# Rewriting a two-layer trunk: feature-major inputs, one feed-forward pass, norms spread between matmuls

## The chip, the cores and the metric

The kernel runs on all 8 cores of one Trainium2 chip (two dies of four cores); each core computes its own tokens and nothing is exchanged. The time is that of the slowest core, in device microseconds (us). Most executions agree within 0.3%. Some fall in a slower state, in which one die shows a lower granted TensorE clock (after's run of 1534.13 us: die 0 at 0.81 to 0.83, die 1 at 0.94 to 0.95); these are marked slow and are left out of every comparison here, or only the cores of the undisturbed die are used. PE is TensorE, PEld its weight loads, DVE VectorE, ACT ScalarE, POOL GpSimd.

## The reference

One step of a diffusion trunk with two layers. Each core has 512 prompt tokens (two requests of 256) and a run of some 1,280 latent tokens with its margins; later stages need fewer of them (1,152, then 1,024).

```python
D_MODEL = 1024; D_FF = 2816; DEPTH = 2; BLOCK = WINDOW = CHUNK = 128

def modulate(x, g, shift, scale):
    return rms_norm(x, g) * (1 + scale) + shift

def conv_ffn(h, w_up, conv_w, w_down):
    z = dwconv3(h @ w_up, conv_w)            # 3 taps along the tokens
    g, val = jnp.split(z, 2, axis=-1)
    return (jax.nn.silu(g) * val) @ w_down

def gmlp_mixer(h, w_in, v_g, w_s, b_s, w_out):
    u, v = jnp.split(jax.nn.gelu(h @ w_in), 2, axis=-1)
    v = rms_norm(v, v_g)                     # then mixed in chunks of 128 tokens
    ...
    return (u * s) @ w_out

# for each layer l:
#   shift, scale, gate (x2) = silu(cond) @ ada_w[l] + ada_b[l]      "modulation maps"
#   layer 0: q,k,v, a short gated conv; windowed attention with sink; out-projection
#   layer 1: gmlp_mixer
#   x = x + gate * mixer(modulate(x, ...))
#   x = x + gate2 * conv_ffn(modulate(x, ...), ...)
```

## The kernel before

Activations are kept feature-major in SBUF, the memory on the core (features on the 128 partitions, 8 chunks of them, tokens along the row). x comes token-major from the host, so TensorE transposes it block by block, and the outputs too:

```python
P.dma("sp", st[0:nt, :], dram(dsrc.ap()[roff + t0:roff + t1, :]))
for half in range(2):
    b = bank()
    for kk in range(4):
        k = half * 4 + kk
        P.transpose(b[:, kk * 128:kk * 128 + nt], st[0:nt, k * 128:(k + 1) * 128], ident[0:nt, 0:nt])
    # ... copy to xT
```

Phases end in a fence: everything after it depends on the last operation of every engine and on all transfers before it. A norm is a stage of its own inside such a phase. For each tile of tokens: squares on ScalarE, the sum over features by a matmul with a matrix of ones, and for each of the 8 chunks a product (x times 1/rms) and an affine (scale and shift):

```python
def norm_mod_batched(l, which, ranges, sqs, rstd_all, tmps, part="both"):
    # ... squares, sums, Ln and Exp for every tile, then for each tile:
        for k in range(KC):
            tm = tmps[(k % 2) * 2 + (k // 2) % 2]
            if k % 2 == 0:
                P.tt("dve", tm[:, 0:n], xT[:, k, xc:xc + n], rs, ALU.mult)
                P.act(hT[:, k, hc:hc + n], tm[:, 0:n], AF.Identity,
                      bias=mod_ap(l, 3 * which, k, j), scale=gmod[:, l, which, k:k + 1, j])
            else:
                P.tt("pool", tm[:, 0:n], xT[:, k, xc:xc + n], rs, ALU.mult)
                P.ts("dve", hT[:, k, hc:hc + n], tm[:, 0:n], gmod[:, l, which, k:k + 1, j],
                     mod_ap(l, 3 * which, k, j), ALU.mult, ALU.add)
```

Feed-forward runs twice over the up weights, once for each set of at most 900 columns:

```python
for si, st in enumerate(sts):              # two sets of tiles
    for s in range(nslab):                 # up weights read again for each set
        # ... per tile: 8 + 8 matmuls (gate, value), then
        P.act(tg[:, 0:n], bg[:, 1:n + 1], AF.Identity, scale=fcw[:, l, j, 1:2])
        P.act(tv[:, 0:n], bv[:, 1:n + 1], AF.Identity, scale=fcw[:, l, NFC + j, 1:2])
        P.stt("dve", tg[:, 0:n], bg[:, 0:n], fcw[:, l, j, 0:1], tg[:, 0:n], ALU.mult, ALU.add)
        # ... three more taps on VectorE
        if pending is not None:
            stage_b(pending)               # Silu on ScalarE, gate * value on GpSimd
```

Of the kernel before, what the change touches and what calls it, by code (L numbers as in the profile page):

```python
# [12 lines left out]

ENGINES = ("pe", "act", "dve", "pool", "sp")

class Acc:
    __slots__ = ("ap", "name", "box")

    def __init__(self, ap, name, box):
        self.ap = ap  # L20
        self.name = name
        self.box = box

class T:
    def __init__(self, handle, name, shape, psum=False):
        self.h = handle
        self.name = name
        self.shape = tuple(shape)
        self.psum = psum

    def __getitem__(self, idx):
        if not isinstance(idx, tuple):
            idx = (idx,)
        box = []
        for d, n in enumerate(self.shape):
            if d < len(idx):
                s = idx[d]
                if isinstance(s, slice):
                    lo = 0 if s.start is None else s.start
                    hi = n if s.stop is None else s.stop  # L40
                    assert s.step in (None, 1)
                else:
                    lo, hi = s, s + 1
            else:
                lo, hi = 0, n
            assert 0 <= lo < hi <= n, (self.name, idx, self.shape)
            box.append((lo, hi))
        if self.psum:
            return Acc(self.h[idx], self.name, None)
        return Acc(self.h[idx], self.name, tuple(box))  # L50
# [4 lines left out]
def reg(acc_like, ap):  # L55
    return Acc(ap, acc_like.name, acc_like.box)

def dram(ap):
    return Acc(ap, "dram:", None)
# [6 lines left out]

def _covers(b1, b2):
# [4 lines left out]

class Op:
    __slots__ = ("idx", "eng", "emit", "deps", "is_dma", "sig", "sem", "semval", "waits")

    def __init__(self, idx, eng, emit, is_dma):
# [3 lines left out]
        self.deps = set()  # L80
        self.is_dma = is_dma
# [3 lines left out]
        self.waits = None  # L85

class Prog:
    def __init__(self, nc):
        self.nc = nc
        self.ops = []  # L90
        self.track = {}
        self.final_dmas = []
        self.fence_deps = set()
        self.fence_last = {}
        self.fence_start = 0

    def fence(self):
        last = dict(self.fence_last)
        dmas = set()
        for op in self.ops[self.fence_start:]:  # L100
            if op.is_dma:
                dmas.add(op.idx)
            else:
                last[op.eng] = op.idx
        self.fence_last = last
        self.fence_deps = set(last.values()) | dmas
        self.fence_start = len(self.ops)

    def add(self, eng, emit, reads=(), writes=(), is_dma=False):
        op = Op(len(self.ops), eng, emit, is_dma)  # L110
        self.ops.append(op)
        op.deps |= self.fence_deps
        reads = [a for a in reads if not a.name.startswith("dram:")]
        writes = [a for a in writes if not a.name.startswith("dram:")]
        for a in list(reads):
            if a.box is None:
                reads.remove(a)
                writes.append(a)
        writes = [Acc(a.ap, a.name, ((0, 1),)) if a.box is None else a for a in writes]
        for a in reads:  # L120
            lst = self.track.setdefault(a.name, [])
            for (box, oi, isw) in lst:
                if isw and _overlap(box, a.box):
                    op.deps.add(oi)
            lst.append((a.box, op.idx, False))
        for a in writes:
            lst = self.track.setdefault(a.name, [])
            keep = []
            for ent in lst:
                box, oi, isw = ent  # L130
# [3 lines left out]
                if _overlap(box, a.box):  # L134
                    op.deps.add(oi)
                    if _covers(a.box, box):
                        continue
                keep.append(ent)
            keep.append((a.box, op.idx, True))
            self.track[a.name] = keep  # L140
        op.deps.discard(op.idx)
        return op
# [5 lines left out]
    def transpose(self, out, in_, ident):  # L148
        return self.add("pe", lambda e: e.transpose(out.ap, in_.ap, ident.ap),  # L149
                        reads=[in_, ident], writes=[out])  # L150

    def act(self, out, in_, func, bias=None, scale=None, accum_out=None):
        reads = [in_]
        kw = {}
        if bias is not None:
            if isinstance(bias, Acc):
                reads.append(bias)
                kw["bias"] = bias.ap
            else:
                kw["bias"] = bias  # L160
        if scale is not None:
            if isinstance(scale, Acc):
                reads.append(scale)
                kw["scale"] = scale.ap
            else:
                kw["scale"] = scale
# [9 lines left out]
    def ts(self, eng, out, in0, s1, s2, op0, op1=None):  # L176
        reads = [in0]
        a1, a2 = s1, s2
        if isinstance(s1, Acc):
            reads.append(s1)  # L180
            a1 = s1.ap
        if isinstance(s2, Acc):
            reads.append(s2)
            a2 = s2.ap
        if op1 is None:
            return self.add(eng, lambda e: e.tensor_scalar(out.ap, in0.ap, a1, a2, op0), reads=reads, writes=[out])
        return self.add(eng, lambda e: e.tensor_scalar(out.ap, in0.ap, a1, a2, op0, op1), reads=reads, writes=[out])  # L187
# [15 lines left out]
    def recip(self, out, in_):  # L203
        return self.add("dve", lambda e: e.reciprocal(out.ap, in_.ap), reads=[in_], writes=[out])  # L204

# [3 lines left out]
    def dma(self, q, out, in_, final=False):  # L209
        op = self.add(q, lambda e: e.dma_start(out.ap, in_.ap), reads=[in_], writes=[out], is_dma=True)  # L210
        if final:
# [3 lines left out]
    def lower(self, sems):  # L215
        ops = self.ops
        per_eng = {e: [] for e in ENGINES}
        for op in ops:
            per_eng[op.eng].append(op)
        waited = {e: {} for e in ENGINES}  # L220
        waited_dma = {e: set() for e in ENGINES}
        for op in ops:
            need_c = {}
            need_d = []
            for d in op.deps:
                p = ops[d]
                if p.is_dma:
                    if d not in waited_dma[op.eng]:
                        need_d.append(d)
                else:  # L230
                    if p.eng == "pe" and op.eng == "pe" and not op.is_dma:
                        continue
                    if need_c.get(p.eng, -1) < d:
                        need_c[p.eng] = d
            w = []
            for pe_, d in need_c.items():
                if waited[op.eng].get(pe_, -1) >= d:
                    continue
                waited[op.eng][pe_] = d
                w.append(d)  # L240
            for d in sorted(need_d):
                waited_dma[op.eng].add(d)
                w.append(d)
            op.waits = w
            for d in w:
                ops[d].sig = True
        for op in ops:
            if op.is_dma:
                op.sig = True
        cnt = {e: 0 for e in ENGINES}  # L250
        dma_rr = {e: 0 for e in ENGINES}
        dma_cnt = {}
        dma_last = {}
        pre_wait = {}
        for op in ops:
            if not op.sig:
                continue
            if op.is_dma:
                pool = sems["dma_" + op.eng]
                k = dma_rr[op.eng] % len(pool)  # L260
                dma_rr[op.eng] += 1
                key = (op.eng, k)
                if key in dma_last:
                    pre_wait[op.idx] = dma_last[key]
                dma_cnt[key] = dma_cnt.get(key, 0) + 16
                op.sem = pool[k]
                op.semval = dma_cnt[key]
                dma_last[key] = (op.sem, op.semval)
            else:
# [3 lines left out]
        self.pre_wait = pre_wait  # L273
        self.per_eng = per_eng
        self.stats = {e: len(per_eng[e]) for e in ENGINES}
        self.stats["sig"] = dict(cnt)

    def emit_engine(self, eng_name, e):
        ops = self.ops
        for op in self.per_eng[eng_name]:  # L280
            if op.idx in self.pre_wait:
                s, v = self.pre_wait[op.idx]
                e.wait_ge(s, v)
            for d in op.waits:
                p = ops[d]
                e.wait_ge(p.sem, p.semval)
# [3 lines left out]
        if eng_name == "sp":  # L290
            for op in self.final_dmas:
                e.wait_ge(op.sem, op.semval)

# [21 lines left out]

D = 1024
KC = 8
NS_IN = 1281
NS_QA = 1280
NS_X1 = 1153  # L320
NS_F0 = 1152
NS_G1 = 1152
NS_F1 = 1024
NPR = 256
EPS = 1e-6
DFF = 2816
NFC = 22

class Seg:
    def __init__(self, name, xc0, hc0, n, cond, vb0):  # L330
        self.name = name
        self.xc0 = xc0
        self.hc0 = hc0
        self.n = n
        self.cond = cond
        self.vb0 = vb0

SEG_S = Seg("s", 0, 1, NS_IN, 0, 0)
SEG_P0 = Seg("p0", NS_IN, NS_IN + 3, NPR, 1, 11)
SEG_P1 = Seg("p1", NS_IN + NPR, NS_IN + 3 + NPR + 2, NPR, 1, 13)  # L340
SEGS = [SEG_S, SEG_P0, SEG_P1]
XC = NS_IN + 2 * NPR
HC = NS_IN + 2 + 2 * (NPR + 2)
NVB = 15
SLOT_G = (0, 2, 1, 3)

def split(n, maxw):
    k = -(-n // maxw)
    base = n // k
    rem = n % k  # L350
    out = []
    t = 0
    for i in range(k):
        w = base + (1 if i < rem else 0)
        out.append((t, t + w))
        t += w
    return out

def seg_tiles(ranges, maxw):
    out = []  # L360
    for seg, n in ranges:
# [994 lines left out]
```

## Time and profile before

1686.21 us, median of 4 runs (1683.61 to 1691.12); all eight cores lie between 1671.3 and 1689.6.

| stage of the kernel before (slowest core) | from, to (us) | us | TensorE busy | granted clock |
|---|---|---|---|---|
| layer 0 up to its feed-forward | 0 to 617 | 617 | 407 | 0.75 |
| feed-forward 0 | 617 to 1016 | 399 | 381 | 0.97 |
| layer 1 mixer with both norms | 1016 to 1285 | 269 | 169 | 0.84 |
| feed-forward 1 | 1285 to 1661 | 376 | 355 | 0.97 |
| output transposes and stores | 1661 to 1690 | 29 | 15 | 0.80 |

These are the windows view of the trace, cut at stage boundaries. In the two feed-forwards TensorE is busy for 381 of 399 and 355 of 376 us at clock 0.97, so there little can be won but by fewer columns; in the first and third rows it is without a matmul for 210 and 100 us, and the prediction reads them more finely. What it calls cold starts shows in the same trace: after 32.05 us of idle time TensorE's matmuls had a granted clock of 0.50 from 1062 to 1066 us, and 1.00 from 1068 on.

### The profile page before, as it was taken

Reading aid. Unit: us, or ns where it says so; the run is one execution under the profiler, and the core shown is the slowest. Engines: PE = TensorE matmul, PEld = TensorE weight load, DVE = VectorE, ACT = ScalarE, POOL = GpSimd, SP = SyncE. Lnnn points to the kernel's source line nnn. Section 1 sums busy time; section 2 is a strip of 40 time slices with the busy share of each in tenths; the row PEclk is TensorE's granted clock in tenths of the full one; section 3 lists DMA queues with packets and bytes.
Section 4 is the critical chain, followed back from the end, with each engine's and each line's share of the span. In section 5 each row is a group of like instructions: output and inputs, shape, how many; then the busy total and the mean of one; then the engine's idle time right before and its main releaser. Section 6 shows DMA issues by size and latency. Waiting matters only on the chain.

```text
span 1689.6 us, 29214 instructions; the slowest of 8 cores (1671.3 to 1689.6 us)
## 1 busy us (share of the span) xinstructions
PE 1326.6 (79%) x9098; PEld 843.4 (50%) x9118; DVE 904.7 (54%) x1690; ACT 728.0 (43%) x1468; POOL 463.9 (27%) x506
## 2 busy tenths in 40 slices
PE   2432658979987957999999991886845899999996
PEld 2320226632222733556677770543523566777775
DVE  3135223566765655971799514124447683489812
ACT  1153444246654453640566306468054461256501
POOL 1025420013330232440344203113124342244400
PEclk9985668975555977999999996899887899999998
DMA  9995003315653048657835160320307756964153
GB/s 183 194 143 70 0 1 51 51 18 84 101 100 51 2 54 115 101 76 102 123 64 76 24 97 0 82 51 1 51 0 88 120 87 91 125 96 79 26 69 150
DMA packets 128321, 126.55 MB, mean 75 GB/s; under 512 B 4513, under 2 KB 107689, under 8 KB 128170
## 3 DMA queue, kind: packets, MB, share of 16 engines
q0 software_dynamic: 121392, 108.93, 44.4%
q1 hardware_dynamic: 6778, 15.76, 2.8%
q8 instruction: 76, 1.25, 0.3%
q14 instruction: 75, 0.61, 0.1%
HBM read 226.79 MB, written 6.82 MB: 138 GB/s over the span
## 4 chain that ended last, share of the span: by engine, by line
PE 58%; DMA 15%; DVE 10%; issue 8%; ACT 7%; POOL 1%; DVEq 0%; SPq 0%; ACTq 0%; POOLq 0%
PE ps_b L145 57%; DMA sb_wslab<-w_up 7%; DVE sb_hT L187 3%; DMA sb_xst<-xs 3%; DMA sb_xst<-xp 1%; DVE sb_tq L204 1%; PE ps_b L149 1%; DVE sb_tmpf L195 1%; DMA sb_wslab<-ada_w 1%; ACT sb_junk L171 1%; DMA sb_wdn<-w_down 1%; DVE sb_tg L174 1%; ACT sb_tq L171 1%; DMA ys<-sb_yst 1%; DVE sb_tmpa L174 1%
## 5 line engine op out<-in xcount | busy, mean ns | idle before, releaser
L145 PE MATMUL ps_b<-sb_hT,sb_wslab 128*128 128x258 bf16 (+7 forms) x4520 | 678.4, 314 | 103.1 <-ACT sb_hT L171 61.6
L145 PEld LDWEIGHTS ps_b<-sb_hT,sb_wslab 128*128 128x128 bf16 x4520 | 450.7, 100 | 326.4 <-issue 137.5
L195 DVE SCALAR_TENSOR_TENSOR sb_tmpf<-ps_b,sb_fcw,sb_tmpf 128x256 f32<-128x256 f32 (+3 forms) x880 | 450.8, 547 | 102.2 <-ACT sb_tmpf L171 55.2
L171 ACT ACTIVATE sb_tmpf<-ps_b,sb_fcw 128x256 f32<-128x256 f32 (+3 forms) x440 | 232.0, 528 | 343.6 <-PE ps_b L145 207.2
L174 POOL TENSOR_TENSOR sb_actT<-sb_tmpf,sb_tmpf 128x256 bf16<-128x256 f32 (+3 forms) x220 | 190.7, 867 | 316.1 <-ACT sb_tmpf L171 222.1
L145 PE MATMUL ps_b<-sb_actT,sb_wdn 128*128 128x256 bf16 (+3 forms) x1760 | 242.4, 301 | 4.2 <-DMA sb_wdn<-w_down 2.3
L145 PEld LDWEIGHTS ps_b<-sb_actT,sb_wdn 128*128 128x128 bf16 x1760 | 172.1, 98 | 74.1 <-issue 5.7
L195 DVE SCALAR_TENSOR_TENSOR sb_xT<-ps_b,sb_modv,sb_xT 128x256 f32<-128x256 f32 (+5 forms) x168 | 88.0, 539 | 216.6 <-PE ps_b L145 216.6
L171 ACT ACTIVATE sb_PT<-ps_b 128x256 bf16<-128x256 f32 x308 | 100.0, 382 | 65.4 <-PE ps_b L145 61.6
L171 ACT ACTIVATE sb_tmpf<-sb_tmpf 128x256 f32<-128x256 f32 (+3 forms) x220 | 101.2, 460 | 2.3 <-DVE sb_tmpf L195 2.3
L204 DVE RECIPROCAL sb_tq<-ps_b 64x512 f32<-64x512 f32 x20 | 67.2, 3360 | 38.8 <-PE ps_b L145 38.7
L174 POOL TENSOR_TENSOR sb_PT<-sb_PT,sb_masks 128x512 bf16<-128x512 bf16 (+1 forms) x38 | 43.8, 1154 | 140.6 <-PE ps_b L145 76.9
L171 ACT ACTIVATE sb_hT<-sb_tmpa,sb_modv,sb_gmod 128x256 bf16<-128x256 f32 (+7 forms) x88 | 56.3, 640 | 59.3 <-DVE sb_tmpa L174 58.3
L149 PE MATMUL ps_b<-sb_ident,sb_xst 128*128 128x128 f32 (+1 forms) x120 | 28.1, 412 | 60.3 <-DMA sb_xst<-xs 44.0
L210 POOL DMA_DIRECT2D sb_wdn<-w_down x16 | 21.9, 1367 | 154.5 <-PE ps_b L145 149.7
L145 PE MATMUL ps_b<-sb_wslab,sb_hT 128*128 128x512 bf16 (+2 forms) x322 | 54.9, 329 | 0.3
L149 PEld LDWEIGHTS ps_b<-sb_ident,sb_xst 128*128 128x128 f32 (+1 forms) x120 | 22.9, 223 | 64.1 <-issue 64.1
L204 DVE RECIPROCAL sb_ssq<-sb_ssq 128x1 f32<-128x1 f32 x13 | 2.1, 164 | 92.8 <-ACT sb_ssq L171 92.8
L171 ACT ACTIVATE sb_sqb<-sb_xT 128x2560 bf16<-128x2560 f32 (+3 forms) x9 | 20.3, 2291 | 65.3 <-issue 64.2
L145 PE MATMUL ps_b<-sb_mixT,sb_wslab 128*128 128x288 bf16 (+2 forms) x384 | 48.0, 287 | 0.0
L145 PE MATMUL ps_b<-sb_uT,sb_wslab 128*128 128x384 bf16 (+1 forms) x320 | 47.7, 313 | 0.0
L145 PE MATMUL ps_b<-sb_PT,sb_Vtok 128*128 128x512 bf16 (+1 forms) x68 | 39.5, 582 | 8.9 <-ACT sb_PT L171 7.1
(163 smaller groups left out, 1184.9 us busy)
## 6 DMA issues: line engine op xcount, KB each, us to landing
sb_wslab<-w_up POOLq DMA_DIRECT2D x40, 1024.0 KB, 13.7
sb_wslab<-ada_w POOLq DMA_DIRECT2D x12, 2048.0 KB, 17.1
sb_wdn<-w_down POOLq DMA_DIRECT2D x16, 1408.0 KB, 14.3
sb_xst<-xs SPq DMA_DIRECT2D x10, 512.0 KB, 9.1
sb_wslab<-w_up POOLq DMA_DIRECT2D x8, 512.0 KB, 6.9
sb_wslab<-w_in_odd POOLq DMA_DIRECT2D x2, 2048.0 KB, 20.1
ys<-sb_yst SPq DMA_DIRECT2D x8, 512.0 KB, 2.7
sb_wslab<-w_in_even POOLq DMA_DIRECT2D x6, 512.0 KB, 9.1
```

What stands on the lines that cost most here:

```text
L145: return self.add("pe", lambda e: e.matmul(out.ap, lhsT.ap, rhs.ap, start=start, stop=stop), reads=[lhsT, rhs], writes=[out])
L149: return self.add("pe", lambda e: e.transpose(out.ap, in_.ap, ident.ap), reads=[in_, ident], writes=[out])
L171: return self.add("act", lambda e: e.activation(out.ap, in_.ap, func, **kw), reads=reads, writes=writes)
L174: return self.add(eng, lambda e: e.tensor_tensor(out.ap, in0.ap, in1.ap, op), reads=[in0, in1], writes=[out])
L187: return self.add(eng, lambda e: e.tensor_scalar(out.ap, in0.ap, a1, a2, op0, op1), reads=reads, writes=[out])
L195: return self.add(eng, lambda e: e.scalar_tensor_tensor(out.ap, in0.ap, sc, in1.ap, op0, op1), reads=reads, writes=[out])
L204: return self.add("dve", lambda e: e.reciprocal(out.ap, in_.ap), reads=[in_], writes=[out])
L210: op = self.add(q, lambda e: e.dma_start(out.ap, in_.ap), reads=[in_], writes=[out], is_dma=True)
```

## The change

Its intent: take away what keeps TensorE empty (transposes, norm stages, fences, the second reading of the up weights), so that it runs from one projection to the next.

The diff has 2,616 lines and is a rewrite. SP is the tile of the prompt, S0 to S3 are the latent tiles; the modulation maps are read and computed in slices (`ada`), like the weights. Its core:

```diff
-    def fence(self):                       # all engines, all transfers
+    # dependencies per buffer and range; no fences
...
-    P.transpose(b[:, kk * 128:kk * 128 + nt], st[0:nt, ...], ident[...])
+    P.dma("sp", xP.whole(), dr(d_xp.ap()))      # x, k cache, outputs feature-major in DRAM
...
-    P.recip(den[64:128, :], OD[64:128, :])
+    P.act(d[:, 0:w], d[:, 0:w], AF.Ln)
+    P.act(d[:, 0:w], d[:, 0:w], AF.Exp, scale=-1.0)
...
+    def unit(key, shape, src, at=None):    # weights: slices, contiguous per partition,
+        ...                                # through one ring of 40,960 bytes a partition, in program order
+    for m in (2, 3, 4):
+        ada_units(0, m)
+    for c in range(8):
+        unit(("we", c), [128, KC, 128], d_we.ap()[c])
...
-    norm_mod_batched(...)                  # a stage of its own
+    def queue_apply(nm):
+        side.append(nm.fin)                # Ln, Exp: 1/rms
+        for k in range(KC):
+            side.append(lambda k=k: nm.apply(k, E1[k], E2[k]))   # product, then affine
+
+    E1 = ("dve", "pool", "dve", "pool", "dve", "dve", "pool", "dve")
+    E2 = ("act", "dve", "act", "act", "act", "dve", "act", "act")
+
+    def emit(f, nside=0):                  # one item of matmul work
+        cur = lag[:]
+        del lag[:]
+        f()
+        for c in cur:                      # what the item before left behind: norm sums
+            c()
+        for _ in range(nside):             # and nside steps of a waiting norm
+            if side:
+                side.popleft()()
+        pump()                             # free ring places, issue weights
...
-    for si, st in enumerate(sts):          # two passes
+    for j in range(NJA):                   # NJA = 6: the first slices, prompt and first tile,
+        for st in sts[0]:                  # carry the norm of the other two tiles
+            emit(lambda: up_item(j, st), 2)
+    side_all()
+    ...
+    for j in range(NJA, NFC):              # then all four tiles, and map slices of layer 1
+        for st in sts[0] + sts[1]:
+            emit(lambda: up_item(j, st))
...
+    acc = 0.0
+    rate = n_fill / (len(un) - 6.0)        # attention: filler is meant to be mixed in,
+    for i in range(len(un) + 2):           # but acc never grows
+        ...
+        while acc >= 1.0:
+            acc -= 1.0
+            if fill:
+                emit(fill.popleft())
```

## The prediction

> **What bounds the kernel now.** I read the page's slices first, then the windows view cut at the stages that the chain of waits names, then finer windows, the groups by form, and the timeline inside the attention.
>
> ```profile
> PE   2432658979987957999999991886845899999996
> PEclk9985668975555977999999996899887899999998
> ```
>
> One digit is 42 us. TensorE is full in two long stretches, 617 to 1016 us and 1285 to 1661 us (the two feed-forward layers), and part idle elsewhere. Its granted clock is about half between slices 9 and 13. The stages:
>
> ```profile
> core 6: us, PE busy (x) PEld busy (x) DVE busy (x) ACT busy (x) POOL busy (x), PEclk, DMA share, GB/s
> 0.00:130.00 130.00, 47.70 (x552) 39.21 (x552) 39.36 (x60) 36.00 (x43) 20.37 (x29) 0.93 0.93 169
> 130.00:275.00 145.00, 78.05 (x380) 40.50 (x381) 45.61 (x95) 65.08 (x150) 52.13 (x55) 0.65 0.21 28
> 275.00:350.00 75.00, 72.87 (x470) 45.15 (x469) 41.05 (x73) 19.72 (x38) 0.88 (x1) 1.00 0.27 43
> 350.00:565.00 215.00, 176.98 (x1066) 66.90 (x1078) 138.59 (x240) 117.85 (x335) 54.04 (x50) 0.59 0.43 69
> 565.00:617.00 52.00, 31.22 (x242) 23.96 (x243) 31.80 (x68) 25.23 (x35) 18.34 (x23) 0.84 0.00 1
> 617.00:1016.00 399.00, 381.15 (x2632) 258.08 (x2629) 255.43 (x480) 160.25 (x331) 126.56 (x139) 0.97 0.62 88
> 1016.00:1062.00 46.00, 8.65 (x42) 4.47 (x43) 24.77 (x41) 30.26 (x32) 18.74 (x20) 0.61 0.00 0
> 1062.00:1110.00 48.00, 47.95 (x321) 32.10 (x320) 0.00 (x0) 18.86 (x40) 1.51 (x2) 0.94 0.35 72
> 1110.00:1188.00 78.00, 51.82 (x298) 24.77 (x302) 31.76 (x60) 65.45 (x91) 25.20 (x23) 0.97 0.16 28
> 1188.00:1238.00 50.00, 48.46 (x328) 32.48 (x328) 25.36 (x45) 0.00 (x0) 6.13 (x6) 0.94 0.27 43
> 1238.00:1285.00 47.00, 12.03 (x56) 6.55 (x57) 24.56 (x42) 29.31 (x33) 20.78 (x24) 0.65 0.01 1
> 1285.00:1661.00 376.00, 355.10 (x2625) 256.46 (x2623) 237.72 (x479) 153.06 (x330) 119.22 (x137) 0.97 0.63 88
> 1661.00:1690.00 29.00, 14.61 (x96) 12.78 (x96) 8.68 (x13) 6.93 (x12) 0.00 (x0) 0.80 0.53 218
> ```
>
> In order: load and transposes; norm and q, k, v; short conv; attention; out-projection with norm; feed-forward 0; norm; u; v and spatial gate; out-projection; norm; feed-forward 1; output transposes. Three norm stages and the load leave TensorE nearly empty, attention has it "busy" at half clock, and the feed-forward is TensorE's own time. For that time:
>
> ```profile
> 20.00:40.00 20.00, 7.85 (x90) 6.64 (x88) 2.98 (x6) 1.93 (x4) 0.88 (x1) 1.00 1.05 218
> ...
> 680.00:700.00 20.00, 20.00 (x124) 11.85 (x122) 18.36 (x31) 11.99 (x23) 8.79 (x10) 1.00 0.68 105
> ```
>
> Second line: 124 matmuls of 386 columns in 20 us are 161 ns each, that is columns/2.4 and no more. VectorE is at 92% there, but TensorE is the one that is never idle. First line: DMA is saturated at the start. Inside the attention:
>
> ```profile
> 429.61 0.40 PE L145 MATMUL ps_b<-sb_mixT,sb_KTd 64*128 64x256 bf16 x2 [0.47 <-issue]
> ...
> 429.94 0.61 PE L145 MATMUL ps_b<-sb_PT,sb_Vc 128*128 128x512 bf16 x1
> 430.15 0.66 ACT L171 ACTIVATE sb_PT<-ps_b 128x256 bf16<-128x256 f32 x2 [0.23 <-PE ps_b L145]
> ...
> 430.48 0.39 PE L145 MATMUL ps_b<-sb_mixT,sb_KTd 64*128 64x256 bf16 x2
> ```
>
> The two 64-row score matmuls run side by side (two in 0.40 us). One unit takes 0.87 us: 256 + 512 columns at half clock are 0.64 us, and each of the two switches loses 0.11.
>
> ```profile
> L195 DVE SCALAR_TENSOR_TENSOR sb_tmpf<-ps_b,sb_fcw,sb_tmpf 128x256 f32<-128x256 f32 x352 | 158.3, 479 | 19.8 <-ACT sb_tmpf L171 0.9 <-DVE sb_tmpf L195 0.5
> L195 DVE SCALAR_TENSOR_TENSOR sb_tmpf<-ps_b,sb_fcw,sb_tmpf 128x384 f32<-128x384 f32 x264 | 157.2, 615 | 41.1 <-ACT sb_tmpf L171 27.0
> ```
>
> A conv tap costs 479 ns at 256 and 615 at 384, so 1.06 ns an element and 207 fixed.
>
> [...] this trace, on eight cores, shows 1.00 through 100 us and more of dense matmuls, so I use 2.4 GHz. [...] in the first 60 us some 11.5 MB landed, about 2.6 MB of it x in f32, the rest bf16 weights read as f32 at twice the size, so 20.4 MB in 57 us or about 358 GB/s (my estimate)[...]. [...] here exp takes 382 ns at 256 elements and gelu 595 at 512, which is 0.832.
>
> **The change part by part.** It is a rewrite. x, k cache and outputs come feature-major from the host, so all TensorE transposes go; weights come in slices that are contiguous for each partition, in a small ring; the prompt is one 512-column tile; feed-forward runs once over all 1664 columns, so up weights are read once, not twice; phase fences are replaced by dependencies per buffer; norms are spread between matmuls of the neighbouring stage; layer 1's and layer 0's last modulation maps move into feed-forward 0; the 3.36 us reciprocal becomes Ln and Exp; a unit of attention holds both key heads. The loop meant to mix filler work into attention never increases its counter, and the attention holds all eight banks: attention runs alone and the filler after it.
>
> Start. Before q, k, v can begin, xP 2.1, xS0 1.6, small ones 0.5 and two modulation maps of 4.2 MB each have to be read, then rotary tables, cache and kv weights 3.6 MB beside xS1 1.6 MB: 17.8 MB at 350 GB/s is 51 us, plus 5 until the first transfer: first projection at about 55, against some 155 now.
>
> q, k, v and half the conv. Columns: k 14k, q 53k, v 15k, block sums and rotations 14k, norm sums 7k, half the conv 80k: 184k, 77 us at 2.4 GHz. The first third (prompt, S0, three norms) is held by the others: per rotary chunk POOL two products of 1.0 us, and VectorE and ScalarE 1.8 each, plus a norm's 5 us on VectorE for each tile; I put 40 us there and 60 for the rest, which TensorE sets. Attention starts at about 157.
>
> Attention. 70 units of 512 (the pair of scores) + 1024 columns. At half clock 1.28 us + two switches of 0.11 = 1.5 us; ScalarE needs [...] 1.02 us of exp, and 1.2 of Ln and Exp per seven units, so 1.2. The 62 latent units at 1.5 make 93. The four prompt blocks have two units each but one normalise buffer: VectorE 2.7, ScalarE 1.2, POOL 1.3 and waits, near 5.5 us a block, 22 together[...]. Plus filling, 118, to 275.
>
> Filler. Second half of the conv 33, twelve map slices of 16 matmuls at 26 ns (64 take 1.70 us in the chain of waits) 5, out-projection of the prompt and S0 57k columns 24. The last four slices find no room in the ring before the last conv weights are free: 4.2 MB then, some 14 us with TensorE waiting. With cold starts 80; the single token's attention and S1, S2's out-projection (49k columns, 20.5) 25 more: feed-forward 0 starts at 380.
>
> Feed-forward 0. Up 22 x 16 x 1669 columns = 245 us, with 1 ns a matmul 246.5; 28 map slices 12; down 176 x 1664 = 122.7; norm sums 5.7; sum 387. VectorE per slice of four tiles: 4 x 750 + 12 x 615 = 10.4 us, under TensorE's 11.2, but the first six slices also carry two norms: 4 us lost. 391, against 399.
>
> Layer 1. u 98k columns 41; v 13 chunks of 16 x 512 44 and spatial products 104 at about 100 ns 11; out-projection 41; norm sums 5; 8 us of gaps: 150, against 269 for the five stages before.
>
> Feed-forward 1: 352 x 1541 + 176 x 1536 columns, 341, and 4 lost: 345, against 376. Last transfer 5, against 29.
>
> Sum: 157 + 118 + 105 + 391 + 150 + 345 + 5 = 1271; I say 1275.
>
> **Rivals.** One, VectorE becomes the bound of feed-forward: 93% of TensorE's time in a slice. For it: semaphore waits add to that, and norms and map slices pile on. Against it: before, 92% left TensorE full. If it holds, 22 slices lose about 1 us in each layer: 1320. Two, attention stays warm: VectorE no longer stalls it by 3.36 us reciprocals, and the v stage kept clock 0.97 with TensorE busy 52 of 78 us; then ScalarE's 1.2 us a unit sets it: 62 x 1.2 + 16, and 25 to 28 us less, 1247. [...] Four, weight transfer: map slices and up weights need 3.15 MB per 12 us, 262 GB/s, under 350; packets that do worse than I think would stall feed-forward 0 by some 20 us.
>
> **Range and chances.** The feed-forward and layer 1 (891 of the sum) are TensorE columns and may miss by 20; layer 0 until 380 rests on chained estimates and may miss by 40, more likely upward. 1220 to 1340. The change would have to lose 400 us to miss 2%: faster 0.98, same 0.01, slower 0.01.
>
> **What would show it.** First q, k, v matmul near 55 us; attention 115 us long at clock about 0.5 with nothing else on TensorE; a wait for map slices of 10 to 15 us after the conv; feed-forward windows with TensorE at 20.00 of 20 and clock 1.00; no stretch over 10 us without TensorE in layer 1. Wrong if feed-forward lasts over 410, if the start is over 80, or if the clock in dense windows is below 0.95.

## The result, and the profile after

After: 1383.64 us, median of 10 runs (1381.03 to 1534.13; two of them slow). Before, in the same rounds: 1686.97, median of 16. Ratio of the fast runs 0.8198, 95% interval 0.8187 to 0.8208. A ratio is the mean time of one kernel's fast runs over that of the other's of the same rounds, so it isn't quite the ratio of the medians. The outputs are correct. The change is 303 us faster, and 109 us slower than the predicted 1275, outside the range of 1220 to 1340.

The page of the profile after, TensorE's busy tenths and clock in 40 slices of 34.6 us:

```profile
PE   0455967787877899999999997996876999999999
PEclk8677988898889899999999999997999999999999
```

The full stretches have grown (slices 14 to 23 and 31 to 39), but most of slices 1 to 13 are still loose, and some of slices 24 to 30. The windows view of after, cut at the same stages as the table of before, without the last 4 us (columns: window, its length, busy time with instruction counts of PE, PEld, DVE, ACT, POOL, then clock, DMA share, GB/s):

```profile
0.00:423.00 423.00, 278.94 (x1649) 126.41 (x1664) 187.09 (x335) 199.10 (x313) 102.00 (x124) 0.83 0.41 76
423.00:833.00 410.00, 393.07 (x2566) 221.70 (x2592) 257.56 (x449) 184.96 (x332) 142.03 (x167) 0.98 0.52 92
833.00:1018.00 185.00, 153.54 (x846) 81.68 (x859) 93.15 (x125) 84.47 (x143) 55.22 (x55) 0.92 0.25 45
1018.00:1378.00 360.00, 344.77 (x2080) 203.69 (x2105) 229.54 (x397) 147.15 (x283) 108.03 (x123) 1.00 0.36 69
```

| stage | before | predicted | after | after minus predicted |
|---|---|---|---|---|
| first projection starts | ~155 | 55 | 58 | +3 |
| q, k, v and half the conv | | 102 | 129 | +27 |
| attention | | 118 | 111 | -7 |
| filler, out-projections, to feed-forward 0 | | 105 | 125 | +20 |
| *layer 0 up to its feed-forward* | *617* | *380* | *423* | *+43* |
| feed-forward 0 | 399 | 391 | 410 | +19 |
| layer 1 mixer | 269 | 150 | 185 | +35 |
| feed-forward 1 | 376 | 345 | 360 | +15 |
| end | 29 | 5 | 4 | -1 |

Of the 308 us between the two profiled executions 194 come from layer 0 up to its feed-forward and 84 from layer 1; feed-forward 0 is 11 us longer than before, where it had neither norms nor maps beside it. Finer windows of after show where the predicted sum was short:

```profile
76.00:123.00 47.00, 21.25 (x104) 10.60 (x105) 23.28 (x39) 23.36 (x47) 17.24 (x18) 0.68 0.40 92
123.00:187.00 64.00, 57.07 (x359) 32.31 (x359) 38.38 (x71) 29.44 (x60) 21.51 (x23) 0.97 0.00 1
187.00:298.00 111.00, 78.28 (x275) 17.24 (x281) 47.71 (x86) 81.55 (x94) 20.65 (x22) 0.80 0.19 29
...
380.00:423.00 43.00, 34.12 (x187) 17.29 (x187) 19.71 (x35) 20.12 (x39) 9.99 (x11) 0.88 0.22 38
423.00:485.00 62.00, 48.24 (x232) 23.93 (x236) 37.97 (x59) 33.68 (x56) 17.16 (x17) 0.89 0.05 9
485.00:702.00 217.00, 215.69 (x1608) 126.16 (x1623) 187.10 (x341) 120.92 (x224) 104.13 (x121) 1.00 0.65 115
...
935.00:985.00 50.00, 37.27 (x180) 18.01 (x180) 23.48 (x33) 11.39 (x20) 15.57 (x16) 0.80 0.23 43
...
1018.00:1081.00 63.00, 49.10 (x269) 25.25 (x271) 41.81 (x69) 35.27 (x62) 19.23 (x19) 1.00 0.00 1
```

The dense part of feed-forward 0 (485 to 702) is what was predicted: TensorE 99% busy at clock 1.00, with VectorE at 86%. The loose rows, attention (187 to 298) apart, are the ones that have a norm beside them: the start (76 to 123), the second out-projection of layer 0 (380 to 423), the first slices of both feed-forwards (423 to 485, 1018 to 1081) and the out-projection of layer 1 (935 to 985). In none of them is any engine full: between 423 and 485 VectorE, the busiest after TensorE, has 38 of 62 us. So it is not an engine's throughput that is short; it is an order of waits. The timeline of after inside that window (start, duration, engine, operation; in brackets the idle time before it and what ended that):

```profile
440.56 1.24 ACT L215 ACTIVATE ft<-ps,cf 128x512 f32<-128x512 f32 x2
441.33 3.11 DVE L239 SCALAR_TENSOR_TENSOR ft<-ps,cf,ft 128x510 f32<-128x510 f32 x4 [1.48 <-ACT ft L215]
441.70 0.52 ACT L215 ACTIVATE ft<-ft 128x384 f32<-128x384 f32 x1
442.36 1.00 POOL L218 TENSOR_TENSOR actT_a<-ft,ft 128x384 bf16<-128x384 f32 x1 [3.56 <-ACT ft L215]
443.32 1.00 POOL L218 TENSOR_TENSOR tB<-xS,rB 128x384 f32<-128x384 f32 x1
...
444.41 1.31 ACT L215 ACTIVATE hS<-tB,modv,gmod 128x384 bf16<-128x384 f32 x2 [2.19 <-POOL tB L218]
445.62 1.02 ACT L215 ACTIVATE ft<-ps,cf 128x384 f32<-128x384 f32 x2
...
449.49 0.71 ACT L215 ACTIVATE hS<-tB,modv,gmod 128x384 bf16<-128x384 f32 x1 [2.32 <-POOL tB L218]
...
450.11 1.24 ACT L215 ACTIVATE ft<-ps,cf 128x512 f32<-128x512 f32 x2
450.87 3.11 DVE L239 SCALAR_TENSOR_TENSOR ft<-ps,cf,ft 128x510 f32<-128x510 f32 x4 [0.48 <-ACT ft L215]
...
452.62 3.70 PE L199 MATMUL ps<-hS,w_up 128*128 128x385 bf16 x11 [9.14 <-DVE ft L239]
```

Read it as a ring. ScalarE runs the Silu of the tile before (441.70). GpSimd's gate product waits for it (442.36), and the norm's product stands behind the gate product in GpSimd's queue (443.32). ScalarE's next instruction is the affine of that product, so ScalarE stands idle for 2.19 us until 444.41, and the evictions of the tile whose matmuls are already done come after it (445.62). An eviction here is ScalarE's first reading of a matmul's result. VectorE's taps (the conv) come after it, and only then is the PSUM bank free, one of the kernel's eight buffers for the results of matmuls. The same happens once more for the next tile (affine at 449.49 after an idle time of 2.32 us, evictions at 450.11, taps at 450.87), and at 452.62, when two of these taps are done, TensorE has waited 9.14 us for a bank. ScalarE kept the order of its queue here: it ran nothing in those 2.19 us, though the matmuls of the eviction that came at 445.62 had ended at 440.

Something else has a share in those 9.14 us. `take` in the kernel hands out free bank number i modulo the number of free banks. A norm reserves one bank until its 1/rms is computed; when it gives the bank back, the modulus changes and the count jumps. Replayed from the kernel, the two returns of a bank in these slices put the two tiles that wait here (2.63 us at 429.50 and 9.14 at 452.62) on banks that the tile just before had filled. At the second, the tile three before had its taps done by 444.44, so its banks were free. The ring says how late a tile's banks come free; that TensorE waits for just these is the allocator's choice. No run changed it, so how the loss in feed-forward 0 divides between the two is open.

The wait for weights that the prediction named is there as well. One piece of the chain that ended last, in after (start, us, what; `w_we` are the out-projection's weights of layer 0):

```profile
337.86 14.82 DMA w_we<-w_oe
```

### The profile page after: what moved, and what is told of

Its sections match the earlier page's. It is cut to its first block, busy times and chain, and to the rows that moved or that the text cites. A ratio compares the mean times of both kernels' runs of the same rounds, so it can differ in the third digit from the quotient of the medians.

```text
span 1382.2 us, 21358 instructions; the slowest of 8 cores (1371.4 to 1382.2 us)
## 1 busy us (share of the span) xinstructions
PE 1171.5 (85%) x7147; PEld 634.1 (46%) x7225; DVE 767.9 (56%) x1307; ACT 615.7 (45%) x1070; POOL 407.3 (29%) x469
## 4 chain that ended last, share of the span: by engine, by line
PE 68%; DVE 9%; ACT 8%; issue 6%; DMA 6%; POOL 3%; DVEq 0%; ACTq 0%; POOLq 0%; SPq 0%
PE ps L199 68%; DVE ft L239 3%; DMA xS<-xs 3%; DMA w_ada<-ada 2%; ACT ft L215 2%; ACT pt L1009 2%; ACT hS L215 1%; DVE nd L218 1%; DMA w_we<-w_oe 1%; ACT L215 1%; DVE xS L239 1%; ACT nd L215 1%; POOL actT_a L218 1%; DVE xP L239 0%; ACT hP L215 0%
## 5 line engine op out<-in xcount | busy, mean ns | idle before, releaser
L239 DVE SCALAR_TENSOR_TENSOR ft<-ps,cf,ft 128x510 f32<-128x510 f32 (+5 forms) x704 | 419.2, 630 | 86.1 <-ACT ft L215 46.3
L199 PE MATMUL ps<-hS,w_up 128*128 128x386 bf16 (+4 forms) x2112 | 340.5, 321 | 25.8 <-DVE ft L239 23.2
L199 PEld LDWEIGHTS ps<-hS,w_up 128*128 128x128 bf16 x2112 | 205.3, 98 | 160.0 <-issue 39.1
L215 ACT ACTIVATE ft<-ps,cf 128x384 f32<-128x384 f32 (+4 forms) x354 | 201.9, 589 | 131.4 <-PE ps L199 128.8
L218 POOL TENSOR_TENSOR actT_a<-ft,ft 128x512 bf16<-128x512 f32 (+2 forms) x96 | 99.0, 1031 | 191.3 <-ACT ft L215 128.2
L199 PE MATMUL ps<-hP,w_up 128*128 128x512 bf16 x666 | 151.0, 379 | 4.1 <-DVE ft L239 1.6
L199 PE MATMUL ps<-actT_a,w_dn 128*128 128x384 bf16 (+4 forms) x761 | 139.7, 333 | 1.2 <-DVE xS L239 0.8
L218 POOL TENSOR_TENSOR actT_b<-ft,ft 128x512 bf16<-128x512 f32 (+2 forms) x80 | 82.5, 1031 | 121.6 <-ACT ft L215 107.7
L199 PE MATMUL ps<-actT_b,w_dn 128*128 128x384 bf16 (+4 forms) x634 | 118.1, 333 | 0.3
L215 ACT ACTIVATE ft<-ft 128x384 f32<-128x384 f32 (+4 forms) x178 | 94.6, 531 | 53.1 <-DVE ft L239 52.7
```

Of the source, the lines that this page charges most:

```text
L199: return self.add("pe", lambda e: e.matmul(out.ap, lhsT.ap, rhs.ap, start=start, stop=stop), reads=[lhsT, rhs], writes=[out])
L215: return self.add("act", lambda e: e.activation(out.ap, in_.ap, func, **kw), reads=reads, writes=writes)
L218: return self.add(eng, lambda e: e.tensor_tensor(out.ap, in0.ap, in1.ap, op), reads=[in0, in1], writes=[out])
L239: return self.add(eng, lambda e: e.scalar_tensor_tensor(out.ap, in0.ap, sc, in1.ap, op0, op1), reads=reads, writes=[out])
```

## The experiments

Eleven kernels ran, all on one chip (it isn't recorded whether it is that of the result above). There one die, mostly die 1, was sometimes at a lower clock (in the slowest of these runs, 1514.20 us, die 1 at 0.82 to 0.84 and die 0 at 0.94 to 0.95), so I compare ratios of fast runs, or the cores of die 0 where that die was undisturbed. Before took 1695.88, 1686.40 and 1694.29 us in the three calls; the median core of its die 0 took 1674 to 1681 in all of them (means 1676.6 to 1676.9), so die 0 compares across calls. All stage times below are of core 0. The letters of the theories are those of the texts: A, the in-order queues described above; B, VectorE's throughput; C, TensorE's wait in the out-projections for the square of the chunk just made; D, conv weights that are read ahead of the second latent tile S1; E, the order of the norms' steps in the start; F and G are told with their runs.

**Control.** After, unchanged.

> The changed kernel once more, unchanged, so that this chip's own time, its clock and its cores are known beside the other three. About 0.82 of the kernel before (1384 us on the first chip).

1383.82 us, ratio 0.8208 (0.8195 to 0.8220). The experiments' ratios stand against this one.

**Affines two chunks behind their products.**

```diff
-            for k in range(KC):
-                side.append(lambda k=k: nm.apply(k, E1[k], E2[k]))
+            for k in range(KC + 2):        # step k: affine of chunk k-2, product of chunk k
+                side.append(lambda k=k: half(k))
```

> Edit: where a norm is applied between matmuls, the affine of chunk k is issued two chunks after its product, so ScalarE no longer stands waiting for a product that VectorE or GpSimd has still in its queue. Work of every engine is unchanged. Theory A (the lost time beside the feed-forward is a loop of in-order queues: ScalarE's affine waits for GpSimd's product, that waits behind the gate product, that waits for ScalarE's Silu): the first six up slices, 62 us in layer 0 and 63 in layer 1 where the matmuls need about 36 and 33, fall to 45 or less each, and the whole by about 35 us, to some 1350. Theory B (VectorE has too much work there): less than 5 us.

Correct; 1365.34 us, ratio 0.8042 (0.8022 to 0.8063): 0.0166 under the control, about 28 us; by the median core of die 0 (1348 to 1352, control 1372 to 1375) 24. I use 26. Up phase of feed-forward 0 (first up matmul to first down matmul): 276.9 to 271.1; feed-forward 1: 362.7 to 350.9. In the 62 us from the first up matmul, the waits view of the control (engine and what it wrote, what it waited for, us in total, times, longest):

```profile
POOL actT_a L218 <- ACT ft L215: 41.0, 9, 12.4
...
ACT hS L215 <- DVE tB L218: 14.3, 6, 3.4
PE ps L199 <- DVE ft L239: 13.4, 3, 9.2
ACT hS L215 <- POOL tB L218: 6.6, 3, 2.3
```

and of this run, where the last of these is no longer listed:

```profile
POOL actT_a L218 <- ACT ft L215: 26.4, 6, 13.7
...
PE ps L199 <- DVE ft L239: 7.4, 2, 4.8
...
ACT hS L215 <- DVE tB L218: 5.0, 3, 2.1
```

The same instructions in another order: ScalarE waits 5.0 us for products instead of 20.9, and TensorE 7.4 us for banks instead of 13.4. That is theory A. It was less than expected: the first slices still take longer than their matmuls need. In feed-forward 0 TensorE still waits at the two places where the count of banks jumps, only shorter the second time (2.63 and 4.75 us, control 2.64 and 9.15). In the first slices of feed-forward 1, where the replay finds no tile on its predecessor's banks, its waits for taps fell from 11.1 us in all to none: there the order of the queues alone shows.

**All affines on VectorE.**

```diff
-        E2 = ("act", "dve", "act", "act", "act", "dve", "act", "act")
+        E2 = ("dve",) * 8
```

> Edit: all affines of the norms go to VectorE, none to ScalarE: 6 more of 0.48 us in each of 16 norms, 46 us more of VectorE work in all, some 6 us of it in each layer's first up slices. Theory A (in-order loop through ScalarE): the loop is cut at ScalarE, the first six up slices fall from 62 and 63 us to about 50, the whole by 10 to 25 us. Theory B (VectorE throughput): these stretches get longer by the added work, the whole slower by 10 to 30 us.

Correct; 1386.16 us, ratio 0.8176 (0.8161 to 0.8191), 5 us under the control. This fits neither theory: no 10 to 25 us gain and no loss. One of the four runs was slow; by the median core of die 0 (1367 to 1369) it is 6 us. The up phase of feed-forward 0 did not move (278.8; the wait of TensorE at the second jump of the bank count is 10.35 us here, control 9.15); the first pass of u in layer 1 went from 33.3 to 26.8, since ScalarE's gelu no longer stands behind affines there. So the affine's wait seems to move to VectorE's queue where the taps are, and to go where VectorE has nothing else. It also says that VectorE had room: six more affines a norm cost it nothing.

**Norm sums of the out-projections two items later.**

```diff
-                if stat:
+                if stat and deep:                # in the out-projections
+                    lag.append(lambda: lag.append(lambda: nm.stat(k)))
+                elif stat:
                     lag.append(lambda: nm.stat(k))
```

> Edit: in the out-projections the norm-sum matmul of a chunk is issued two items later instead of one. Theory C (TensorE waits there for the residual and the square of the chunk it has just made): a pair of items in layer 1's out-projection falls from 3.83 us to about 3.4, and the three half out-projections that carry norm sums get shorter by 4 to 6 us each, the whole by about 12, to some 1371. Against C (the pace there is set by VectorE's residuals or the eviction of banks): less than 3 us.

Correct; 1380.13 us, but two of its four runs were slow. On die 0, undisturbed in all of them, the median core took 1361 to 1365 us against 1372 to 1375 in the control's fast runs: 12 less. The out-projection of layer 1 went from 77.6 to 67.1 us; that of layer 0 did not change. The windows view of its first 50 us, in the control and then here:

```profile
923.70:973.70 50.00, 36.02 (x195) 18.26 (x196) 23.80 (x34) 12.33 (x22) 15.40 (x16) 0.90 0.22 43
```

```profile
924.00:974.00 50.00, 37.20 (x216) 19.50 (x217) 31.93 (x45) 18.77 (x33) 21.12 (x20) 0.95 0.24 44
```

More of everything gets done in the same 50 us (216 matmuls instead of 195). In after a pair of tiles waited for the square of the chunk just made; here other matmuls lie between.

**Conv weights issued later.**

```diff
         P.dma("sp", xT.whole(), dr(d_xs[3].ap()))
-        for _ in range(4):
-            issue(wq.popleft())                   # the conv's weights; now after the first norms
```

> Edit: the four conv weight loads (6.3 MB of f32 read) are not issued ahead with the first weights but when the first projection is emitted, so they do not share the DMA engines with xS1 and xS2. Theory D (the second latent tile comes at 76 us because weights that are needed at 123 us are read beside it): the norm of S1 starts at about 58 us instead of 76, attention at about 172 instead of 187, the whole falls by about 15 us, to some 1369. Against D (the stretch 76 to 123 us is bound by the loop of queues, whenever its data comes): the start of S1 moves, but attention by less than 5 us.

Correct; 1388.87 us, ratio 0.8210 (0.8169 to 0.8251): nothing. S1's norm began at 73 to 77 us instead of 76 to 77, not at the expected 58. As a test of theory D it is weak: the weights are now issued at 58.7 us, S1 has not landed yet, and DMA stays full (share 1.01 from 58 to 76), so the two are still read side by side. Issued at 9 or at 58.7, they make no difference; what delays S1 is open. In after DMA is full until about 90 us (share 0.99 to 1.01).

**Start of layer 0 in another order.**

```diff
-        tm0 = [... for i in range(2)]
+        tm0 = [... for i in range(4)]             # four product buffers
-            nm.sq(k, ("act", "dve", "pool", "act", ...)[k])
+            nm.sq(k, ("act", "dve", "act", "dve", ...)[k])
-        stats(nmS1)                               # squares, sums, 1/rms in one go
-        emit(lambda: qk_chunk(S0, 4))
-        for k in range(KC):
-            nmS1.apply(k, E1[k], E2[k])
-        emit(lambda: v_blocks(S0, [0, 1, 2]))
+        emit(lambda: qk_chunk(S0, 4))
+        sqs(nmS1)
+        emit(lambda: v_blocks(S0, [0, 1, 2]))
+        emit(lambda: qk_chunk(S0, 0))
+        sums(nmS1)                                # one or two projections after the squares
+        emit(lambda: qk_chunk(S0, 1))
+        papply(nmS1)                              # affines two chunks behind
         ...
```

> Edit in the start of layer 0 alone: the products of the norms of the latent tiles have four buffers instead of two and their affines come two chunks later, no squares on GpSimd, and a tile's norm sums are put on TensorE one or two items after its squares. Theory E (the 65 us between the first projection and the conv, which I had put at 40, are TensorE standing in order behind norm sums and ScalarE and VectorE taking turns over two buffers): that stretch falls to 50 or less, attention starts 12 to 20 us earlier, the whole by as much. Against E (the engines' work or the arrival of x sets it): less than 5 us.

Correct; 1368.02 us, ratio 0.8115 (0.8102 to 0.8129): 16 us under the control. Attention (its first product with the values) starts at 176.2 instead of 189.3. Theory E holds, though which of the three changes does it isn't told apart. The window of the loosest 48 us, in the control and then here:

```profile
76.00:124.00 48.00, 21.12 (x104) 10.51 (x105) 23.28 (x39) 23.47 (x47) 17.40 (x18) 0.69 0.38 90
```

```profile
76.00:124.00 48.00, 25.67 (x134) 13.07 (x134) 31.07 (x55) 28.23 (x58) 19.57 (x21) 0.79 0.38 90
```

There TensorE still idles for nearly half. From the first projection to the first conv matmul it now takes 44 us instead of 66, but from there to attention 71 instead of 62: the products and affines of S2 and S3 were moved into that part. So about 10 of the 22 us won came back.

**The norms' products and affines left out.** Wrong on purpose (relative error 4.7): the steps that are spread beside matmuls are dropped, their squares and sums kept.

```diff
-            for k in range(KC):
-                side.append(lambda k=k: nm.apply(k, E1[k], E2[k]))
```

> Wrong result on purpose: the products and affines of the norms that run beside matmuls (12 tiles of 8 chunks, 96 pairs) are left out, the norm sums stay. It shows the floor that these stretches have without them. If the norm work beside the matmuls is what my sums missed, each layer's up phase falls to within 5 us of its columns (feed-forward 0 from 410 to about 392, 1 from 362 to about 346), u's first pass from 33 to 26, the out-projections by 5 to 10: 50 to 60 us in all. If the losses there are from something else (banks, semaphores, weight transfers), most of them stay, and the whole falls by less than 25.

1336.47 us, ratio 0.7926 (0.7912 to 0.7940): 47 us under the control. So all the products and affines spread beside matmuls together cost 47 us of time (44 by die 0), where the prediction had 4 + 4 and a part of 8. The removal also moves the two returns of a bank next to each other, and TensorE's waits after them in feed-forward 0 shrink to 0.91 and 0.26 us; so the 47 include what the allocator costs. On core 0 the up phase of feed-forward 0 lost 15.4, feed-forward 1 14.7, the first pass of u 6.9, the out-projections 4 and 5.5. One thing is not explained: the down phase of feed-forward 0 was 7.5 us longer.

**All parts together.** The affines' lag, the later sums and the new start; a fourth product buffer in layer 1; and the out-projection's weights ahead of the last four map slices.

```diff
-        for m in (2, 3, 4):
+        for m in (2, 3):
             ada_units(0, m)
         for c in range(8):
             unit(("we", c), [128, KC, 128], d_we.ap()[c])
+        ada_units(0, 4)
```

> A version meant to be faster: affines two chunks after their products everywhere, norm sums of the out-projections two items later, the start as in the run before, a fourth product buffer in layer 1, and the out-projection weights fetched ahead of the last four modulation slices, so that TensorE doesn't stand 16 us for those. If the causes add up: 26 for the affines, 13 for the sums, 12 to 20 for the start, 10 for the weights: some 60 to 70 us under the control, about 1320. If they hide one another (a stretch shortened only makes the next wait longer): 30 to 40.

Correct; 1312.88 us, ratio 0.7781 (0.7766 to 0.7795). That is 71 us under the control (1383.82) of the same rounds, 5% faster than after and 22% faster than before: the best kernel. Two waits at jumps of the bank count (2.99 and 7.91 us, first slices of feed-forward 0) are still in it: the next thing to try. TensorE's busy line of its page (slices of 32.8 us), where only slices 0 and 1 are below six tenths:

```profile
PE   1366967789987999999999997998899999999999
```

**Only the order of the weights.**

```diff
-        for m in (2, 3, 4):
+        for m in (2, 3):
...
+        ada_units(0, 4)                           # after the out-projection's weights
...
+        for q in range(4):                        # and their matmuls after the prompt's and S0's
+            fill.append(lambda q=q: ada_item(0, 4, q))
```

> After, with one thing changed: the out-projection's weights are read ahead of the last four modulation-map slices, and those slices' matmuls come after the out-projection of the prompt and S0. Theory F (transfer order: TensorE waits 14.8 us because the last map slices stand ahead of the out-projection's weights in a ring that is full until the conv is done): the wait goes and the map slices land under 24 us of out-projection, 12 to 15 us less, ratio 0.811 to 0.814, out-projection begins near 330 instead of 346. It would also close the account of the version with all parts (-71 = -26 -12 -16 and about -15 here, 2 for the rest). Rival (the ring is full: whatever is read last is waited for): the same 15 us appear at the map slices, ratio 0.819 to 0.822.

Correct; 1374.48 us, ratio 0.8108 (0.8081 to 0.8134), 17 us under the control; on die 0 13 us. The out-projection starts at 331.9 instead of 346.6. Theory F (the transfer is in the wrong order in a full ring) holds. The wait as the control's windows show it, then the same place here:

```profile
331.00:346.50 15.50, 2.54 (x66) 2.04 (x64) 3.17 (x12) 0.03 (x1) 8.97 (x17) 0.58 0.96 159
```

```profile
332.00:347.00 15.00, 14.89 (x79) 7.69 (x80) 8.10 (x13) 4.63 (x8) 5.82 (x11) 1.00 0.95 144
```

DMA is as full (0.96, 0.95), but TensorE goes from 2.54 us busy to 14.89: the transfer is hidden. Some 3 us come back later: from the out-projection to the first up matmul it takes 69.8 instead of 66.5. With this the account of the version with all parts nearly closes. By the median core of die 0 alone, the one measure that all these runs have, 24 (affines) + 12 (sums) + 12 (start) + 13 (order) are 61 of 68 us (1374 to 1306). The other 7 are the fourth buffer in layer 1, which was not tried alone, or what the parts do to each other.

**All parts, and the affines of u's first pass on VectorE.**

```diff
-        def queue_apply(nm):
+        def queue_apply(nm, E2=E2):
...
         for nm in keepB:
-            queue_apply(nm)
+            queue_apply(nm, ("dve",) * 8)
```

> The version with all parts (1312.88), and in layer 1's first pass of u the affines of the two norms go to VectorE instead of ScalarE. Theory G (there ScalarE also carries the gelu of u, VectorE has nothing else, so the affine is what holds the pass): u pass 33 to 27 us, 1306, ratio 0.774 to 0.775. Rival (the products' own two engines set the pass, as the fourth buffer and the lag changed nothing there): no change, ratio 0.778.

Correct; 1316.36 us, ratio 0.7764 (0.7739 to 0.7789). The pass itself does what theory G said, 33.2 to 27.0 us. In the total it is not resolved: the intervals overlap with those of the version with all parts, and die 1 was longer than die 0 in most of these runs. On die 0 the median core took 1301 to 1305 us against 1305 to 1307, 3 us less.

**All parts, without the norms' products and affines.** Wrong on purpose, as above.

> The version with all parts, wrong on purpose: the products and affines of the norms that are spread beside matmuls are left out, their sums kept. This measures what is left of the norms' cost. In after the same removal gave 47 us. Theory A (most of the cost was the order of the queue, which the affines' lag takes away, 26 us): 18 to 25 us less than the version with all parts, 1288 to 1295, ratio 0.763 to 0.768. Rival (lag and removal act on different costs): still 40 us or more, below 1273, ratio under 0.755.

All nine runs were slow: die 1 at a mean clock of 0.90 to 0.94 and with a median core of 1311 to 1359 us. On die 0 the median core took 1285 to 1292 us, against 1305 to 1307 in the version with all parts: 17 us less, just under the expected 18 to 25. By the same measure the removal gave 44 us in after. So some 17 of the 44 remain, and the other three fifths went with this version's parts, 24 us of them with the lag when it was tried alone.

## Why the prediction was wrong

It was wrong by 109 us, upward, and the direction of the change was right. By its own steps:

- **What failed: the norms spread beside matmuls.** The prediction priced this work by engine throughput: "the first six slices also carry two norms: 4 us lost", "and 4 lost" in feed-forward 1, "8 us of gaps" in layer 1. Its only worry was a full VectorE (rival one), and the engines had room, so the answer was a few us. Measured, the first six slices took some 52 us in feed-forward 0 and 46 in feed-forward 1 where their 6 x 16 x 897 columns need 36 at the measured 161 ns for 386 columns, TensorE waited in the items after them too, and leaving the products and affines out won 47 us in all (with u's pass and the out-projections). The missing term is the wait in a queue that was worked off in order: an affine at the head of ScalarE's queue that wasn't ready (2.19 and 2.32 us in the timeline of after) held the evictions behind it, and these held the banks. The reordered affines, same instructions and same engines, won 26 us; that shows it, most clearly in feed-forward 1. In feed-forward 0 two jumps of the bank count, which the prediction didn't look at, have a share that no run separates. Rival one is refuted: VectorE had 38 of 62 us there and 86% in the dense part, with TensorE at 99%.
- **The start: "I put 40 us there and 60 for the rest".** The 60 were 64. The 40 were 65 (58 to 123). A reordering took that stretch to 44, but put work into the next one, and won 13 us in all; so at least half of the 25 is order and buffers. For the rest no run gives the cause, and the theory on weights ahead of S1 found no support.
- **"S1, S2's out-projection (49k columns, 20.5)".** This was priced by columns alone, 25 us with the single token's attention; it took 43. In layer 1 the out-projection took 83 us (935 to 1018, the last five of the thirteen spatial products with it) where the prediction had 41 for its columns. Later norm sums won 10.5 us of the latter on core 0. In layer 0 they won nothing, so there the cause of the 18 us is only partly known (4 us went with the norms' steps).
- **Right: the feed-forward's columns.** "TensorE's 11.2" a slice plus the map slices: the dense stretch (485 to 702 us) took TensorE's own time, 215.69 of 217 us at clock 1.00.
- **Right: the wait for map slices,** "some 14 us": 14.82 in the chain, and moving the read took it away.
- **Right in size, not in mechanism: attention,** 118 predicted and 111 measured. The prediction had TensorE at half clock, 1.5 us a unit. The clock was 0.80, and in the latent blocks ScalarE sets the pace. The timeline of after around one normalisation:

```profile
240.03 1.35 ACT L215 ACTIVATE nd<-nd 128x512 f32<-128x512 f32 x2 [1.34 <-DVE nd L218]
...
241.29 2.88 ACT L1009 ACTIVATE pt<-ps 128x1024 bf16<-128x1024 f32 x3
...
250.28 1.35 ACT L215 ACTIVATE nd<-nd 128x512 f32<-128x512 f32 x2 [1.33 <-DVE nd L218]
```

  Seven units take 10.25 us (240.03 to 250.28), 1.46 each: seven exponentials of about 1.0, Ln and Exp 1.35, 1.33 of waiting for VectorE and 0.9 for TensorE (two waits in lines left out here). Rival two had "62 x 1.2 + 16"; it was right that the clock is higher, if only in part (0.80 over the attention of after, 0.59 over that of before), and that ScalarE sets the pace, and left out these waits. That the total came out near 118 is luck.
- **Right: the first projection** at 58 for 55, and the end, 4 for 5.
- **A slip in the sum:** 55 + 40 + 60 are 155, and the prediction went on from 157.

What the corrections add up to: 1271 + 47 (norm steps) + 27 (start) + 14 (out-projection of layer 0, without the 4 that the norm steps have) + 12 (sums in layer 1) are 1371, against 1383.64 measured; the other 12 us stay unexplained, and some of the terms are core 0's, some the slowest core's. The range was too narrow on this side because all these terms rest on one assumption, that work beside matmuls is free as long as no engine is full, and the prediction treated their errors as small and separate.

## What to carry to other kernels

Work moved beside a dense stage has to be priced by what stands behind each instruction in its engine's queue, not by the engine's free time: ask what the first instruction that isn't ready holds up, and issue a consumer some steps after its producer (two were tried here). Where three engines hand work to each other in a ring (here Silu, gate product, norm product, affine, eviction), a reordering with no instruction fewer can be worth half of what taking all of the norm work out is worth (26 of 47 us). When TensorE waits for a bank, look up which one: an allocator that hands out the bank just filled, while others are free, can turn a delay in the ring into TensorE's own wait (read here from the kernel and two waits, not tried). In a ring buffer for weights, the order of the reads is part of the schedule: what is read last into a full ring should be what the longest matmul work can hide.

## Two measurements of the hardware

- **The granted clock.** After's profile shows 1.00 over 217 us of dense matmuls (485 to 702, on each of the eight cores). On the chip of the experiments a lower clock came and went, on one die at a time: in the run with late conv weights core 5 (die 1) had 0.99 from 1100 to 1260 us. In the last down phase it had 0.81, and core 0 (die 0) of the same execution 1.00 in the same window:

```profile
1300.00:1320.00 20.00, 20.00 (x88) 9.47 (x87) 2.74 (x4) 0.00 (x0) 1.05 (x2) 0.81 0.56 119
```

```profile
1300.00:1320.00 20.00, 19.89 (x116) 11.37 (x116) 3.29 (x5) 0.00 (x0) 1.06 (x2) 1.00 0.64 132
```

  In the densest kernel (all parts, norms' steps left out) die 1 was slow in nine runs of nine (mean clock 0.90 to 0.94); whether density is the cause was not tested.
- **Two f32 products side by side.** After's timeline shows VectorE's product alone at 0.55 us, and at 1.04 when it began while GpSimd's product (85.57, 1.00 us) was running.

```profile
84.49 0.55 DVE L218 TENSOR_TENSOR tm<-xS,rs 128x384 f32<-128x384 f32 x1
...
85.94 1.04 DVE L218 TENSOR_TENSOR tm<-xS,rs 128x384 f32<-128x384 f32 x1 [0.51 <-ACT hS L215]
```

  So these two took 1.41 us together, and two on VectorE alone took 1.16 (87.89): products split between the two engines gained nothing here.
